# A planner that counts SyncE's own time in an attention stage, and key page tables that borrow the room of later ones

## The chip, the cores and the metric

The kernel runs on one core of a Trainium2 chip. The time is device time of one launch, in microseconds (us), the median of several executions. A profiled execution is a separate one, recorded by the hardware profiler. The engines that the text names are TensorE (PE, with PEld for its weight loads), VectorE (DVE), ScalarE (ACT), GpSimd (POOL) and SyncE (SP), which issues most of the DMA transfers.

## What is computed

One inference step of a two-layer decoder trunk in float32: layer 0 mixes tokens by a Conformer convolution, layer 1 by stick-breaking attention, and each layer ends in a gated ConvFFN. There are 512 prompt tokens and 8 sequences of 4 new tokens each, whose past of 256 tokens lies in 16 pages of a key and value pool. The change touches only the attention:

```python
def stick_breaking_block(q, k, v, bias, q_start):
    z = jnp.einsum('bqhd,bkhd->bhqk', q, k) * (HEAD_DIM ** -0.5) + bias[None, :, None, None]
    valid = k_pos[None, :] < q_pos[:, None]
    log_fail = jnp.where(valid, jax.nn.log_sigmoid(-z), 0.0)
    after = lax.cumsum(log_fail, axis=3, reverse=True) - log_fail
    weights = jnp.where(valid, jnp.exp(jax.nn.log_sigmoid(z) + after), 0.0)
    return jnp.einsum('bhqk,bkhd->bqhd', weights, v)
```

It is called once for the prompt (512 queries against 512 keys, 16 heads of 64) and once for the new tokens (4 queries against 256 paged keys and 4 new ones, for each sequence). New key and value rows are outputs too.

## The kernel before

All activations stay in the chip's memory, channels on the 128 partitions. Each weight block is split into a high and a low float32r part, `whi` by ScalarE and `wlo` by VectorE, and multiplied in three passes: high with high, low with high, high with low.

**The attention stage** is one `Plan`. Code records operations with `plan.op(engine, cost, function, r=reads, w=writes, a=adds)`, and at the end `plan.run()` lists them: it keeps a modelled clock for each engine, and again and again takes the operation that can start first, with corrections for rank and urgency. The instructions are issued in that order, so the costs in the list decide what stands ahead of what on each engine; on the chip each engine then works strictly in this order and waits on semaphores. An operation on SyncE has two times in the model: its cost, after which its readers may start, and the time for which it holds SyncE, which is 0.7 us for every one of them.

What the stage records, for 8 pairs of heads c = 0 to 7:

- `keys(c, h)` and `values(c, h)`, for token halves h: projections (`project`, lines 2163 to 2165 of `weighted`, six matmuls for each quarter), which TensorE uses as filler. Key rows are transposed by VectorE (line 2207) into one of two buffers `kr`, and four transfers of SyncE store them (line 2212). Value rows go through TensorE (line 2193) and a copy (line 2225), and one transfer stores them (line 2228).
- `pair(c)`: the prompt's attention in units of 512 columns. A unit is: logits z on TensorE (line 2432), exponential on ScalarE (2438) into a buffer `e` of a ring of six, masking on GpSimd (2446), clamp on VectorE (2451), logarithm on ScalarE (2453), scans on VectorE (2462), exponential (2466), product on VectorE (2467), transposes on TensorE (2474) with copies (2477), and products with the values (2494).
- `page_logits(m)`, m = 0 to 3: one group of four key pages each. A page is loaded by SyncE in four transfers of 128 KB (`key_page`, line 2045) into one of three page buffers, transposed by VectorE (line 2283), and multiplied with placed queries `Qz` (line 2301). Pages 0 to 2 are there before the stage. The even pages' transposes go to `kt`, the odd pages' to `second`: two of the six `e` buffers.
- `decode_weights`, `sequence(n)`: the new tokens' weights over the pages, and their products with value pages, which GpSimd gathers (line 2050). `new_logits` and `new_weights` do the same for the 4 new keys, from tables `Qf` (queries placed by 32 copies of GpSimd, `place_f`, line 2082), `kn` (keys, line 2315) and `Zw`, `wn` (weights). `Qf` and `Zw` are zeroed before the stage; `place_f` is recorded near its start.

Weight blocks of 1 MB come through SyncE as well (line 361), each into one of two buffers, when VectorE has split the block that was there. Each transfer of SyncE also waits until the one eight places ahead of it on SyncE has landed, since eight completion semaphores are used in turn.

Of the kernel before, what the change touches and what calls it, by code (L numbers as in the profile page):

```python
# [9 lines left out]
F32 = mybir.dt.float32  # L10
# [7 lines left out]
P = 128  # L18
D = 1024
# [62 lines left out]
E_BUFS, S_BUFS = 6, 2  # L82
# [23 lines left out]
class Plan:  # L106
# [5 lines left out]
    def __init__(self, eager=EAGER, chain=0.0, shifts=""):  # L112
        self.eager = eager
        self.shifts = shifts

        self.chain = chain
        self.ops = []
        self.writes, self.adds, self.reads = {}, {}, {}
        self.rings = {}
        self.follows = {}  # L120
        self.lift, self.urgent = {}, {}
        self.forms, self.change = {}, 0.0
        self.fill = set()

    def op(self, eng, cost, fn, r=(), w=(), a=(), follows=None, lift=0.0, urgent=0.0, after=(), form=None):

# [34 lines left out]
        if form is not None:  # L161
            self.forms[i] = form
        return i

# [27 lines left out]
    def run(self):  # L192
# [24 lines left out]
        while any(ready.values()):  # L217
# [23 lines left out]
            last[eng] = i  # L241
            free[eng] = t + (cost if eng != "sp" else 0.7)
            for u in users[i]:
# [7 lines left out]
def tile_trunk(  # L251
# [1866 lines left out]
    new_s = xflat[:, 4 * D:4 * D + 2 * P]  # L2118
    Zw = va.tile([P, 4, P], F32, name="Zw")
    wn = va.tile([P, 4, P], F32, name="wn")  # L2120
    oacc = Zd
    dec = vw.tile([P, NC, 4, 8], F32, name="dec")
    kn = vw.tile([P, NC, NS], F32, name="kn")
    Qf = vw.tile([P, NC, 4 * NS], F32, name="Qf")
    pool.memset(Qf, 0.0)
    pool.memset(Zw, 0.0)
    kt = kT.rearrange("p c t -> p (c t)")[:, 4 * T:4 * T + NC * KW]
# [70 lines left out]
    def keys(c, h):  # L2198
# [15 lines left out]

        plan.op("sp", 7.0, store, r=[kr])

# [14 lines left out]
    def new_rows(src, r, dst):  # L2231
# [15 lines left out]
        plan.op("act", 0.35, lambda: act.copy(new_s, rows()[:, :2 * P]), r=[rows], w=["new", "Qz"])  # L2247
        plan.op("sp", 3.0, store, r=["new"])


    def page(i):

        t = plan.tile("page", PAGE_BUFS, lambda: page_t[i % PAGE_BUFS])
        if i < PAGE_BUFS:
            plan.op("held", 0.0, lambda: None, w=[t])
            return t
        if i < 2 * NB:
            plan.op("sp", 2.0, lambda: key_page(t(), i), w=[t, ("asked", i)])
        else:
            plan.op("pool", 1.05, lambda: gather(t(), i % (2 * NB), cv), w=[t, ("asked", i)])  # L2260
        plan.op(f"page{i}", 6.0 if i < 2 * NB else 4.0, lambda: None, r=[("asked", i)], w=[(t, 1)])
        return t

    zt = {}

    second = [sbuf("e", 1024, E_BUFS) for _ in range(2)]

    plan.op("first pages", 3.0, lambda: None, w=["pages"])

    def page_logits(m):  # L2270
# [7 lines left out]
        for odd in range(2):  # L2278
            for pg in range(2):
                t = page(4 * m + 2 * odd + pg)  # L2280

                def turn(t=t, pg=pg, odd=odd):
                    dve.transpose(second[pg]() if odd else kt[:, pg * D:(pg + 1) * D], t())

                plan.op("dve", 1.25, turn, r=[t, (t, 1), "pages"], w=[("ktq" if odd else "ktp", pg)],
                        a=[second[pg]] if odd else [])

        def logits():
            for odd in range(2):
                b = 2 * (m % 2) + odd  # L2290
                c0 = 32 * b - 16 * odd
                if odd:
                    parts = [(pg * P, P, second[pg]()) for pg in range(2)]
                else:
                    parts = [(0, KW, kt)]
# [8 lines left out]

        plan.op("pe", 1.72, logits, r=[(k, i) for k in ("ktp", "ktq") for i in range(2)] + ["Qz", *second], w=[z], form="c32")
        if m % 2:
# [216 lines left out]
    both_halves(keys, 1)  # L2523
    for bg in range(2):
        plan.op("pool", 5.0, lambda bg=bg: place_f(bg), a=["Qf"])
    both_halves(values, 0)
    for c in range(NC):
# [3 lines left out]
        if c == 2:  # L2531
            decode_weights()
        if c + 2 < NC:
            both_halves(keys, c + 2)
# [89 lines left out]
```

## Time and profile before

| | |
|---|---|
| Median of 3 runs (lowest, highest) | 1257.34 us (1256.36 to 1258.67) |
| The profiled execution's own time | 1256.83 us |
| Its span | 1255.1 us |
| Attention stage, logits of the first unit to the last pair | about 639.6 to 826.5 us |
| DMA over the span | 142.40 MB, mean 113 GB/s |
| Key page loads, q1 and SyncE | 64 transfers of 128 KB |

A row of a window has its start and end, its length, and the busy time of TensorE, its weight loads, VectorE, ScalarE and GpSimd with the number of instructions, then TensorE's granted clock, the DMA engines' busy share and GB/s. A row of a timeline has start, duration, engine, source line, operation, "out<-in" by the program's names, shapes and a count; in brackets stands how long the engine sat idle before it, and what released it. SPq is SyncE's queue of transfers. A row of the chain of waits is one piece of the chain that ended last.

### The profile page before, as it was taken

The numbers are of one execution on the slowest core, as the hardware profiler recorded it, in microseconds if no ns is written. First come the engines' busy times: TensorE is split into PE (matmuls) and PEld (weight loads), VectorE is DVE, ScalarE is ACT, GpSimd is POOL, SyncE is SP. The second block draws the span as 40 slices with busy tenths as digits, with TensorE's granted clock in tenths as the row PEclk, the third lists the DMA queues.
The fourth block names the chain that finished last, engine by engine and source line by source line (L and its number), as shares of the span: only waits on it lengthen the run. The fifth ranks groups of instructions, "written<-read, shape, count | busy, mean of one in ns | idle before, by whom it ended". The sixth has DMA issues, their size and how long they took to land.

```text
span 1255.1 us, 26652 instructions
## 1 busy us (share of the span) xinstructions
PE 1239.3 (99%) x10742; PEld 1187.2 (95%) x10742; DVE 1011.2 (81%) x1700; ACT 709.8 (57%) x1421; POOL 173.8 (14%) x363
## 2 busy tenths in 40 slices
PE   9999999999999999999999999999999999999997
PEld 8997699999999999999988888999999999999997
DVE  7999887988987886878969897646979987887863
ACT  7793584646655454445545887744636645455453
POOL 5000014111001000000242344000101001000000
PEclk9999999999999999999999999999999999999999
DMA  7455423123233233244379465232123232233121
GB/s 223 129 168 152 129 68 117 35 86 114 80 112 118 68 106 99 92 145 161 97 190 246 128 173 159 71 126 85 49 88 102 93 120 93 80 108 118 60 79 72
DMA packets 139661, 142.40 MB, mean 113 GB/s; under 512 B 24045, under 2 KB 132773, under 8 KB 139266
## 3 DMA queue, kind: packets, MB, share of 16 engines
q1 hardware_dynamic: 133134, 120.29, 32.1%
q0 software_dynamic: 6400, 20.41, 5.2%
q8 instruction: 84, 1.38, 0.5%
q14 instruction: 39, 0.32, 0.1%
q10 hardware_dynamic: 4, 0.01, 0.0%
HBM read 129.34 MB, written 12.18 MB: 113 GB/s over the span
## 4 chain that ended last, share of the span: by engine, by line
PE 81%; DVE 14%; DMA 2%; ACT 2%; issue 1%; SPq 0%; POOL 0%; DVEq 0%; ACTq 0%
PE acc L1635 5%; PE acc L1634 5%; PE acc L1633 5%; PE acc L759 4%; PE acc L760 4%; PE acc L761 4%; PE av L896 3%; DVE wlo L401 3%; PE av L1412 3%; PE av L1413 3%; PE av L1414 3%; PE tr L1413 3%; PE tr L1412 3%; PE tr L1414 3%; PE tr L1633 3%; PE tr L1635 3%
## 5 line engine op out<-in xcount | busy, mean ns | idle before, releaser
L398 ACT CAST whi<-raw 128x1024 fp32r<-128x1024 f32 (+2 forms) x247 | 224.7, 913 | 123.5 <-PE av L1413 24.8
L401 DVE TENSOR_TENSOR wlo<-raw,whi 128x1024 fp32r<-128x1024 f32 (+2 forms) x247 | 258.7, 1050 | 33.0 <-ACT whi L398 31.5
L759 PE MATMUL acc<-XH,whi 128*128 128x288 f32 (+1 forms) x384 | 112.7, 294 | 0.0
L761 PE MATMUL acc<-XH,wlo 128*128 128x288 f32 (+1 forms) x384 | 110.3, 287 | 0.9 <-DVE wlo L401 0.9
L760 PE MATMUL acc<-XL,whi 128*128 128x288 f32 (+1 forms) x384 | 110.3, 287 | 0.0
L1412 PE MATMUL av<-HH,whi 128*128 128x288 f32 (+1 forms) x280 | 83.2, 297 | 0.5 <-DVE xT L1735 0.5
L1413 PE MATMUL av<-HL,whi 128*128 128x288 f32 (+1 forms) x280 | 82.6, 295 | 0.0
L1635 PE MATMUL acc<-TH,wlo 128*128 128x272 f32 x288 | 82.6, 287 | 0.0
L1634 PE MATMUL acc<-TL,whi 128*128 128x272 f32 x288 | 82.6, 287 | 0.0
L1633 PE MATMUL acc<-TH,whi 128*128 128x272 f32 x288 | 82.5, 287 | 0.0
L1414 PE MATMUL av<-HH,wlo 128*128 128x288 f32 (+1 forms) x280 | 82.2, 293 | 0.0
L1682 ACT COPY G<-acc 128x272 f32<-128x272 f32 (+1 forms) x72 | 26.8, 372 | 93.8 <-PE acc L1635 93.8
L2163 PE MATMUL acc<-XH,whi 128*128 128x256 f32 (+1 forms) x264 | 79.7, 302 | 0.0
L1412 PE MATMUL tr<-HH,whi 128*128 128x256 f32 (+1 forms) x280 | 78.5, 280 | 0.0
L1413 PE MATMUL tr<-HL,whi 128*128 128x256 f32 (+1 forms) x280 | 78.4, 280 | 0.0
L1414 PE MATMUL tr<-HH,wlo 128*128 128x256 f32 (+1 forms) x280 | 78.3, 280 | 0.0
L2165 PE MATMUL acc<-XH,wlo 128*128 128x256 f32 (+1 forms) x264 | 75.7, 287 | 0.0
L2164 PE MATMUL acc<-XL,whi 128*128 128x256 f32 (+1 forms) x264 | 75.7, 287 | 0.0
L759 PEld LDWEIGHTS acc<-XH,whi 128*128 128x128 f32 x384 | 72.2, 188 | 1.4 <-issue 0.4
L761 PEld LDWEIGHTS acc<-XH,wlo 128*128 128x128 f32 x384 | 72.1, 188 | 1.1 <-DVE wlo L401 1.1
L760 PEld LDWEIGHTS acc<-XL,whi 128*128 128x128 f32 x384 | 72.2, 188 | 0.3
L1573 DVE SCALAR_TENSOR_TENSOR cv<-G,fprm,cv 128x560 f32<-128x560 f32 x88 | 69.5, 797 | 0.5
(464 smaller groups left out, 4343.0 us busy)
## 6 DMA issues: line engine op xcount, KB each, us to landing
raw<-in_ffn_w_gate_dram SPq DMA_DIRECT2D x22, 1024.0 KB
raw<-in_ffn_w_up_dram SPq DMA_DIRECT2D x22, 1024.0 KB
raw<-in_ffn_w_down_dram SPq DMA_DIRECT2D x24, 768.0 KB
raw<-in_attn_w_qkv_dram SPq DMA_DIRECT2D x12, 1024.0 KB
xT<-in_cache_k_dram SPq DMA_DIRECT2D x64, 128.0 KB
raw<-in_conv_w_in_dram POOLq DMA_DIRECT2D x6, 1024.0 KB, 6.8
rep<-glu SPq DMA_DIRECT2D x36, 142.0 KB
raw<-in_conv_w_out_dram POOLq DMA_DIRECT2D x4, 1024.0 KB, 6.4
```

Source lines behind the costliest of these rows:

```text
L398: act.copy(hi[:, k, :], src[:, k])
L401: dve.tensor_tensor(lo[:, k, :], src[:, k], hi[:, k, :], op=ALU.subtract)
L759: pe.matmul(o, hi[:, k, :], XH[:, k, c0:c0 + n], start=(k == 0), stop=False)
L760: pe.matmul(o, hi[:, k, :], XL[:, k, c0:c0 + n], start=False, stop=False)
L761: pe.matmul(o, lo[:, k, :], XH[:, k, c0:c0 + n], start=False, stop=(k == NC - 1))
L1412: pe.matmul(o, hi[:, j + k, :], xh, start=(start and k == 0), stop=False, **kw)
L1413: pe.matmul(o, hi[:, j + k, :], xl, start=False, stop=False, **kw)
L1414: pe.matmul(o, lo[:, j + k, :], xh, start=False, stop=(stop and k == len(xs) - 1), **kw)
L1633: pe.matmul(o, hi[:, j + k, :], xh, start=(start and k == 0), stop=False, **kw)
L1634: pe.matmul(o, hi[:, j + k, :], xl, start=False, stop=False, **kw)
L1635: pe.matmul(o, lo[:, j + k, :], xh, start=False, stop=(k == 3), **kw)
L2163: pe.matmul(o, hi[:, k, :], XH[:, k, c0:c0 + n], start=(k == 0), stop=False)
```

## The change

SyncE's operations get a holding time of their own, `hold`: 2.1 us for a key page, 2.0 for a key row store, 1.9 for the store of new rows, with two of the costs changed too (7.0 to 6.5, 3.0 to 4.0). `Zw` and `wn` become two halves of one table, and the odd key pages' transposes go to that table and to `Qf` in place of two `e` buffers. `Qf` and `Zw` are therefore zeroed, and `Qf` filled, only after the last pages' logits have read them.

```diff
-    def op(self, eng, cost, fn, r=(), w=(), a=(), follows=None, lift=0.0, urgent=0.0, after=(), form=None):
+    def op(self, eng, cost, fn, r=(), w=(), a=(), follows=None, lift=0.0, urgent=0.0, after=(), form=None, hold=0.7):
...
+        self.hold[i] = hold
...
-            free[eng] = t + (cost if eng != "sp" else 0.7)
+            free[eng] = t + (cost if eng != "sp" else self.hold[i])
...
-    Zw = va.tile([P, 4, P], F32, name="Zw")
-    wn = va.tile([P, 4, P], F32, name="wn")
+    Zw_wn = va.tile([P, 8, P], F32, name="Zw_wn")
+    Zw, wn = Zw_wn[:, 0:4, :], Zw_wn[:, 4:8, :]
...
-    pool.memset(Qf, 0.0)
-    pool.memset(Zw, 0.0)
...
-        plan.op("sp", 7.0, store, r=[kr])
+        plan.op("sp", 6.5, store, r=[kr], hold=2.0)
...
-        plan.op("sp", 3.0, store, r=["new"])
+        plan.op("sp", 4.0, store, r=["new"], hold=1.9)
...
-            plan.op("sp", 2.0, lambda: key_page(t(), i), w=[t, ("asked", i)])
+            plan.op("sp", 2.0, lambda: key_page(t(), i), w=[t, ("asked", i)], hold=2.1)
...
-    second = [sbuf("e", 1024, E_BUFS) for _ in range(2)]
+    second = [Zw_wn.rearrange("p a r -> p (a r)"), Qf.rearrange("p k r -> p (k r)")]
...
-                    dve.transpose(second[pg]() if odd else kt[:, pg * D:(pg + 1) * D], t())
-
-                plan.op("dve", 1.25, turn, r=[t, (t, 1), "pages"], w=[("ktq" if odd else "ktp", pg)],
-                        a=[second[pg]] if odd else [])
+                    dve.transpose(second[pg] if odd else kt[:, pg * D:(pg + 1) * D], t())
+
+                plan.op("dve", 1.25, turn, r=[t, (t, 1), "pages"], w=[("ktq" if odd else "ktp", pg)])
...
-    for bg in range(2):
-        plan.op("pool", 5.0, lambda bg=bg: place_f(bg), a=["Qf"])
     both_halves(values, 0)
...
             decode_weights()
+            plan.op("pool", 1.0, lambda: pool.memset(Qf, 0.0), w=[("ktq", 1), "Qf"])
+            plan.op("pool", 0.7, lambda: pool.memset(Zw, 0.0), w=[("ktq", 0)] + [("Zw", i) for i in range(4)])
+            for bg in range(2):
+                plan.op("pool", 5.0, lambda bg=bg: place_f(bg), a=["Qf"])
```

The list that comes out is another one from the first unit on, on every engine, with the same operations in it; line numbers rise by two up to line 2116 and differ by little behind it. First, SyncE and VectorE where key pages 3 to 8 come in. SyncE before (one page is four pairs of an address computation and a load; their repeats are left out):

```order
L2045 ISA
L2045 DMA xT<-in_cache_k_dram 32x4x256
...
L2212 DMA out_dram<-kr_8353 32x8x32 x4
L361 DMA raw_8377<-in_attn_w_qkv_dram 128x8x256
L2212 DMA out_dram<-kr_8364 32x8x32 x4
...
L2212 DMA out_dram<-kr_8455 32x8x32 x4
L2212 DMA out_dram<-kr_8502 32x8x32 x4
```

SyncE now, from the same page loads (3 and 4) on; page 5 stands between the weights and the stores:

```order
L2047 ISA
L2047 DMA xT<-in_cache_k_dram 32x4x256
...
L363 DMA raw_8341<-in_attn_w_qkv_dram 128x8x256
...
L2212 DMA out_dram<-kr_8317 32x8x32 x4
L2212 DMA out_dram<-kr_8332 32x8x32 x4
```

Behind these two stores five pages (6 to 10) follow with no store between them, and no further store comes before page 15, the last. Before, page 5 and 6 stood behind the second store, then came two stores, pages 7 to 10, a fifth store, and the rest.

VectorE before, from the transposes of key rows on (`e_8421` takes page 3, `kT` pages 4 and 5, then `e_8338` page 6):

```order
L2207 STREAM_TRANSPOSE kr_8364<-kT 128x256
L401 TENSOR_TENSOR wlo_8362<-raw_8157,whi_8361 128x1024
L2283 STREAM_TRANSPOSE e_8421<-xT 128x1024
L2207 STREAM_TRANSPOSE kr_8455<-kT 128x256
L401 TENSOR_TENSOR wlo_8449<-raw_8200,whi_8448 128x1024
L2207 STREAM_TRANSPOSE kr_8502<-kT 128x256
L2451 TENSOR_SCALAR e_8467<-e_8467 128x1024
L2283 STREAM_TRANSPOSE kT<-xT 128x1024 x2
L2225 COPY vtok_8238<-one_8514 128x256
L2462 SCALAR_TENSOR_TENSOR s_8512<-ones,s_8512 128x512
L2283 STREAM_TRANSPOSE e_8338<-xT 128x1024
```

VectorE now, from the same place (`Qf` takes page 3, `Zw_wn` page 6; `e_8365` is the first unit, `e_8452` the second):

```order
L2207 STREAM_TRANSPOSE kr_8332<-kT 128x256
L403 TENSOR_TENSOR wlo_8326<-raw_8157,whi_8325 128x1024
L2450 TENSOR_SCALAR e_8365<-e_8365 128x1024
L2283 STREAM_TRANSPOSE Qf<-xT 128x1024
L2461 SCALAR_TENSOR_TENSOR s_8397<-ones,s_8397 128x512 x2
L403 TENSOR_TENSOR wlo_8416<-raw_8200,whi_8415 128x1024
L2283 STREAM_TRANSPOSE kT<-xT 128x1024 x2
L2450 TENSOR_SCALAR e_8452<-e_8452 128x1024
L2466 TENSOR_TENSOR e_8365<-e_8365,s_8397 128x1024
L2225 COPY vtok_8238<-one_8513 128x256
L2461 SCALAR_TENSOR_TENSOR s_8507<-ones,s_8507 128x384
L2283 STREAM_TRANSPOSE Zw_wn<-xT 128x1024
```

The first unit's clamp, scans and product have moved ahead of pages 4 to 6, and the third and fourth transposes of key rows have gone behind all pages. Between page 6's transpose and page 7's there now stand three scans and two clamps.

Second, TensorE from the first page group's logits to the first unit's transposes. Projection matmuls (line 2163 and the next two) stand between these rows and are left out. Before, 48 of them stand ahead of the first row, 30 each ahead of the second line-2193 group and of line 2474, and the second page group comes 6 projections and one z group later:

```order
L2301 MATMUL dz_8477<-kT,xT 32x256 x8
L2301 MATMUL dz_8477<-e_8338,xT 32x128 x4
L2193 MATMUL one_8514<-ident,vT_8505 128x128 x2
...
L2193 MATMUL one_8580<-ident,vT_8573 128x128 x2
...
L2474 MATMUL t_8641<-ident,e_8467 128x128 x4
```

Now 30 projections and a z group stand ahead of it, then 24, 6, 18 and 12 between the rows, and the second page group (last row) comes behind both halves of the first unit's transposes:

```order
L2300 MATMUL dz_8426<-kT,xT 32x256 x8
L2300 MATMUL dz_8426<-Zw_wn,xT 32x128 x4
L2193 MATMUL one_8513<-ident,vT_8504 128x128 x2
L2473 MATMUL t_8523<-ident,e_8365 128x128 x4
L2473 MATMUL t_8535<-ident,e_8365 128x128 x4
L2193 MATMUL one_8579<-ident,vT_8572 128x128 x2
...
L2300 MATMUL dz_8426<-kT,xT 32x256 x8
```

Between the two page groups there are 66 projections before and 60 now; over the whole stage their runs number 49 in both.

Third, GpSimd where the queries for the new keys are placed. Before, at the start of the stage (`kn` is the table of new keys, the maskings are those of the first two units):

```order
L2126 MEMSET Zw 128x512
L2082 COPY Qf<-qT 32x2x4x4 x32
L2315 COPY kn<-kT_s 32x32 x8
L2446 AFFINE_SELECT e_8467<-e_8467 128x2x128
L2446 AFFINE_SELECT e_8536<-e_8536 128x2x128 x2
```

Now, behind the last key page's transpose, among the value gathers (`e_9055` and `e_9278` are units of the third and fourth pair):

```order
L2052 DMA xT<-in_cache_v_dram,idx 128x1024
L2530 MEMSET Qf 128x1024
L2445 AFFINE_SELECT e_9055<-e_9055 128x2x128 x2
L2084 COPY Qf<-qT 32x2x4x4 x32
L2531 MEMSET Zw_wn 128x512
L2445 AFFINE_SELECT e_9278<-e_9278 128x2x128
L2052 DMA xT<-in_cache_v_dram,idx 128x1024 x2
```

The block of 32 copies has moved from ahead of the first masking to between two maskings of later units, behind the third gather of a value page.

More of the change, by code (lines that the diff above doesn't have):

```diff
@@ L123, in __init__ @@
         self.fill = set()
-    def op(self, eng, cost, fn, r=(), w=(), a=(), follows=None, lift=0.0, urgent=0.0, after=(), form=None):
+        self.hold = {}
+    def op(self, eng, cost, fn, r=(), w=(), a=(), follows=None, lift=0.0, urgent=0.0, after=(), form=None, hold=0.7):
         i = len(self.ops)
@@ L2292, in logits @@
                 if odd:
-                    parts = [(pg * P, P, second[pg]()) for pg in range(2)]
+                    parts = [(pg * P, P, second[pg]) for pg in range(2)]
                 else:
@@ L2303, in logits @@
                                       start=(b == e == 0), stop=(b == 3 and e == 1), skip_group_check=True)
-        plan.op("pe", 1.72, logits, r=[(k, i) for k in ("ktp", "ktq") for i in range(2)] + ["Qz", *second], w=[z], form="c32")
+        plan.op("pe", 1.72, logits, r=[(k, i) for k in ("ktp", "ktq") for i in range(2)] + ["Qz"], w=[z], form="c32")
         if m % 2:
```

## The prediction

> **What bounds the kernel now.** I read the engine totals first, then the stretches of the attention stage, then TensorE's waits, then the chain of waits. The first row is the page's, the next four are windows of the trace (the span of each, then busy time and instructions of each engine, granted clock, DMA share, GB/s).
>
> ```profile
> PE 1239.3 (99%) x10742; PEld 1187.2 (95%) x10742; DVE 1011.2 (81%) x1700; ACT 709.8 (57%) x1421; POOL 173.8 (14%) x363
> 639.60:696.00 56.40, 53.55 (x529) 47.48 (x528) 43.65 (x54) 27.48 (x51) 19.37 (x58) 1.00 0.91 219
> 696.00:780.00 84.00, 83.64 (x811) 69.43 (x811) 74.11 (x102) 70.38 (x118) 37.44 (x47) 1.00 0.52 154
> 780.00:826.50 46.50, 45.82 (x555) 41.07 (x553) 29.12 (x53) 32.00 (x65) 2.82 (x9) 1.00 0.33 89
> 826.50:833.00 6.50, 6.20 (x52) 5.95 (x50) 2.49 (x8) 1.52 (x5) 0.42 (x2) 1.00 0.53 225
> ```
>
> TensorE is busy 99% of the span at full clock, so the kernel takes the sum of its matmuls plus its waits. The order outside the attention stage does not change, so only the four stretches count. TensorE idles 56.40 - 53.55 = 2.85 us while the key pages come in, then 0.36, 0.68 and 0.30 us. All of it is 4.2 us, or 0.33% of the time: that is the most that better order can win, and it is little more than the 0.2% (2.5 us) that a measurement of this kernel can tell from no change. The waits by name (total, times, longest):
>
> ```profile
> PE t L2474 <- DVE e L2467: 1.4, 1, 1.4
> PE one L2193 <- ACT vT_s L2223: 1.4, 1, 1.4
> PE t L2474 <- ACT e L2477: 0.7, 1, 0.7
> PE one L2193 <- ACT vT L2221: 0.4, 1, 0.4
> ```
>
> Both long ones lie at 655 and 662 us. The chain of waits says what they come from:
>
> ```profile
> 640.11 5.27 DMA xT<-in_cache_k_dram
> 645.40 0.63 SPq L2212
> ...
> 647.20 4.65 DMA out_dram<-kr
> 652.08 0.27 issue
> 652.35 0.66 DVE e L2451
> ...
> 661.09 1.39 DVE e L2467
> 662.52 0.66 PE t L2474 x4
> ```
>
> A page load lands 5.27 us after its issue; only then does SyncE issue a key row store at 645.40, eight transfers behind that load. The store lands at 651.85, VectorE's next key row transpose waits for it, and the clamp L2451 of the first attention unit stands behind that transpose. So the table of 0.7 us for any SyncE operation hid a real cost, and the change addresses the right place.
>
> **The change, part by part.** *The counted time.* These are SyncE's issues and, last, the time from issue to landing of the page loads:
>
> ```profile
> 637.14 4.73 SPq L2045 DMA_DIRECT2D xT<-in_cache_k_dram  x8
> 642.06 2.22 SPq L2212 DMA_DIRECT2D out_dram<-kr  x4
> 656.98 6.05 SPq L2045 DMA_DIRECT2D xT<-in_cache_k_dram  x12
> DMA to landing us min/median/max: 4.5/5.4/7.7
> ```
>
> A page (four loads) holds SyncE 4.73 / 2 = 2.4 us, or 6.05 / 3 = 2.0; a key row store 2.2. The new 2.1 and 2.0 fit, and this part costs nothing by itself. What it does is order. No transfer is added; SyncE merely defers the stores, three of them past the last page.
>
> *The tables.* Odd pages no longer take two of the six "e" buffers, so the first units start without waiting for them, and the 32 copies of new queries into Qf leave the start of the stage. They held GpSimd for 9.77 us (row below), and the first unit's masking came behind them:
>
> ```profile
> 646.87 0.41 POOL L2446 TENSOR_SCALAR_AFFINE_SELECT e<-e 128x256 f32<-128x256 f32 x1 [0.27 <-POOL kn L2315]
> 640.00:650.00 10.00, 10.00 (x110) 8.21 (x106) 3.92 (x5) 3.06 (x7) 6.09 (x24) 1.00 1.11 258
> ```
>
> The clamp of that unit can now stand ahead of page 3's transpose instead of at 652.35, some 9 us earlier. VectorE was busy 3.92 of the 10 us from 640, so this work is hidden there.
>
> *TensorE's own work.* Over the stage each group of matmuls is still there once, and the number of runs of projection matmuls (49) is the same, so I take no change in the sum, with 0.1 us per moved group either way as a bound (some ten groups: 1 us). Prices come from the distances between these starts, and from the chain of waits:
>
> ```profile
> 636.75 0.28 PE L2163 MATMUL acc<-XH,whi 128*128 128x256 f32 x1
> ...
> 639.64 1.13 PE L2432 MATMUL z<-kT,qT 64*128 64x512 f32 x4
> 640.70 0.40 PE L2163 MATMUL acc<-XH,whi 128*128 128x288 f32 x1
> ...
> 643.97 0.28 PE L2163 MATMUL acc<-XH,whi 128*128 128x256 f32 x1
> ...
> 646.86 1.07 PE L2301 MATMUL dz<-kT,xT 128*32 128x256 f32 x16
> ...
> 665.04 1.87 PE dz L2301 x48
> ...
> 696.08 1.87 PE dz L2301 x48
> ```
>
> 24 projection matmuls take 2.9 us (256 columns) or 3.3 us (288), a group of logits z 1.06 us, the logits of one page group 1.87 us. The first page group is to start after 30 matmuls and a z group, at 640.70 + 3.3 + 0.7 + 1.06 = 645.8, 1.1 us sooner. It needs page 3's transpose, which ended at 644.03 + 1.25 = 645.28: no wait.
>
> From its end (647.6) to the second page group, before, lay 665.04 - 648.7 = 16.3 us with 2.85 of waits, so 13.5 of work. The new order has six projections fewer there (-0.7) and four transposes more (about +0.4): 13.2 us, so TensorE arrives at 660.8. Is VectorE done with page 7 by then?
>
> ```profile
> 644.03 1.25 DVE L2283 STREAM_TRANSPOSE e<-xT 128x1024 f32<-128x1024 f32 x1 [2.91 <-DMA xT<-in_cache_k_dram]
> ...
> 663.55 2.39 DVE L2462 TENSOR_TENSOR_SCAN s<-ones,s 128x384 f32<-128x384 f32 x4
> L2283 DVE STREAM_TRANSPOSE e<-xT 128x1024 f32<-128x1024 f32 x7 | 8.6, 1233 | 5.2 <-DMA xT<-in_cache_k_dram 5.2
> L401 DVE TENSOR_TENSOR wlo<-raw,whi 128x1024 fp32r<-128x1024 f32 x6 | 7.2, 1203 | 0.0
> L2467 DVE TENSOR_TENSOR e<-e,s 128x1024 f32<-128x1024 f32 x4 | 5.1, 1268 | 0.0
> L2451 DVE TENSOR_SCALAR e<-e 128x1024 f32<-128x1024 f32 x4 | 2.6, 662 | 0.0
> ```
>
> SyncE first, with no more than eight transfers under way. Pages 3 and 4 as before, to 641.9; the weights at 642.1; page 5's loads one by one as page 3's land, 642.7 to 644.5; the first store behind page 4's landings, 645.4 to 647.4; the second behind page 5's, 648.2 to 650.0; page 6 behind the first store's landings (4.65 us each), 650.6 to 652.2. At 5.2 us, between the shortest and the median, page 6 has landed by 657.4. On VectorE then come its transpose (1.23), three scans (2.39 less the first, 1.5), two clamps (1.32) and page 7's transpose (1.23): 662.7. **TensorE waits 1.9 us at the second page group.** The bounds are 0, if VectorE finds page 6 as soon as it is through with its earlier work (about 654.4, so 659.7 for page 7), and 4, if page 6 takes the longest 7.7 us. I take 1.9, since 5.2 is nearest to the rows of this stretch. The first unit's transposes cost about 0.2 us more (TensorE is there at 652.8, after a z group and 30 projections; the product, behind page 5's transpose at 651, a clamp and its own 1.27, ends at 653). That is 2.1 for 2.85: **-0.75 us**.
>
> [...]
>
> The third and fourth page groups have slack by the same count: the fourth comes to about 694.2, for 696.08, with about 0.9 us of TensorE work moved behind it. Two terms then remain. **The third pair's transposes** stand 15.8 us of TensorE work behind the fourth page group, at 710.0; on VectorE their product has 25 instructions ahead of it after page 15's transpose (692.5 to 693). At the mean of the stretch, 74.11 / 102 = 0.73 us, it ends at about 711.5; summed by its own kinds, nearer 709.5. Bounds 0 and 1.5, taken 0.4. **The moved Qf block** needs rows of GpSimd:
>
> ```profile
> 634.88 9.77 POOL L2082 COPY Qf<-qT 32x32 f32<-32x32 f32 x32
> 666.76 4.85 POOL L2077 COPY xT<-qT 32x32 f32<-32x32 f32 x16
> ...
> 693.10 0.70 POOL L2315 COPY kn<-kT_s 32x32 f32<-32x32 f32 x3 [6.46 <-DMA xT<-in_cache_v_dram,idx]
> ...
> 762.70 2.55 POOL L2315 COPY kn<-kT_s 32x32 f32<-32x32 f32 x4
> ```
>
> Copies behind a value gather wait for its landing (6.46 us at 693.10); the block now stands behind the third gather, which needs page 15's transpose. So 31 copies begin at about 692.7 + 6.5 = 699.2. At 0.31 us each (9.77 / 32) they end at 708.7, at 0.64 (2.55 / 4) at 719.0; 0.9 us for the fill of Zw and one masking follow. VectorE wants that masking after 31 instructions, at 692.5 + 31 x 0.73 = 715. I take 0.42 a copy, between the 0.30 of 666.76 and 0.64: done by 713.1, no cost. Bounds 0 and 4.9.
>
> Sum: -0.75 + 0.4 = -0.35 us; the 0.36, 0.68 and 0.30 stay, since the order behind the new logits is nearly the same and the last unit's chain does not shift against TensorE. The profiled run took 1256.83 us (span 1255.1), so 1256.5; it lies 0.5 below the median of 1257.34, so **1257.0 us** in the median.
>
> **Rivals.** *A, all the planned waits go (0.29).* Pages 6 and 7 find the DMA queues emptier, with three stores gone from the stretch, where the DMA share is 0.91, and VectorE, some 6 us ahead in its work, is not late again. For it: the 12 loads from 656.98 were issued 0.5 us apart, so the ninth at 661.0 had the first landed after 4.1 us. Then 2.85 + 0.36 go: 1257.34 - 3.2 = **1254.1 us**, faster.
>
> *B, the moved block is late (0.15): slower.* It decides from about 0.5 us a copy on; at 0.64 the masking comes at 719.9 against 715, VectorE stalls, and TensorE, whose next transposes have some 0.5 us of slack, loses 4.4: **1261.4 us**. For it: VectorE is busy 74 of 84 us in that stretch. Against it: the 16 copies at 666.76 ran at 0.30 us with VectorE full. The Trainium skill speaks for it: "SBUF — State Buffer", section "SBUF: two separate sides", says that VectorE and GpSimd share one port pair under an exclusive lock for a whole instruction. The trace agrees in part, with copies of 0.20 us and one of 1.19:
>
> ```profile
> L2082 POOL COPY Qf<-qT x32: 201/205/1187, 634.9 to 644.4; 32x32 f32<-32x32 f32 x32
> ```
>
> *C, the counted time is not the one that limits (0.10).* What paces SyncE is the landing eight transfers back, not 2.1 us of issue. If pages 6 and 7 take 7.7 us, the second page group waits 4.2 instead of 1.9, and VectorE carries some of it to the third: -0.35 + 2.5 + 0.7 is +2.9, **1260.2 us**.
>
> **How the numbers follow.** Forecast 0.46, A 0.29, B 0.15, C 0.10. Faster by over 0.2%: A and 0.02 of the forecast, 0.31. Slower: B and C, 0.25. Within: 0.44. The likeliest case alone spans the bounds of its terms, 1255 to 1259.3. The range takes in A with the 0.68 and some of the moved groups' gain (1253.2), and C and most of B (1261.2); about 2 in 10 is left out.
>
> **What would show it.** In the profile after: the clamp of the first unit before 645 us and no key row wait at 649 to 652 (if it is still there, the counted time failed); the second page group near 662.7 with a wait on L2283 of about 2 us (none: A; 4 and more: C); VectorE without a masking wait of over 1 us near 715 (more: B), and the 32 copies over 20 us there. I am wrong altogether if TensorE's idle time in the stage stays but the time moves, since then the sum of its matmuls changed with the order.

## The result, and the profile after

The changed kernel takes **1265.89 us** (median of 5 runs, 1265.47 to 1268.40) beside 1257.47 for the kernel before in the same session: ratio 1.0071, 95% interval 1.0059 to 1.0083. That is slower by 8.4 us and lies outside the predicted range of 1253.2 to 1261.2. The profiled execution of the changed kernel has a span of 1264.2 us, 9.1 more than before.

First the engine totals of the page, and two windows of the trace after (the first two of the four stretches that the prediction shows; columns as there):

```profile
PE 1243.0 (98%) x10742; PEld 1190.0 (94%) x10742; DVE 1010.7 (80%) x1700; ACT 709.7 (56%) x1421; POOL 174.7 (14%) x363
639.60:696.00 56.40, 52.98 (x514) 45.62 (x513) 48.68 (x56) 34.51 (x57) 16.57 (x38) 0.97 0.87 210
696.00:780.00 84.00, 80.05 (x775) 66.81 (x774) 62.67 (x92) 60.03 (x105) 44.45 (x78) 0.98 0.57 164
```

Two things are new. TensorE idles 3.42 us in the first stretch (2.85 before) and 3.95 in the second (0.36 before), and its granted clock, 1.00 everywhere before, is 0.97 and 0.98 there. So its busy time grew by 3.7 us although it has the same 10742 matmuls. The first logits z of the stage start at 640.73, 1.09 us later than before. That part of the 9.1 is no sign of the new order: `before_b5` below, which differs from the kernel before only behind that point, has its first z at 640.63.

The waits of TensorE by name (total, times, longest):

```profile
PE t L2473 <- DVE e L2466: 3.4, 1, 3.4
PE t L2473 <- ACT e L2476: 2.9, 2, 2.2
PE acc L499 <- DVE xT L2578: 1.3, 1, 1.3
PE av L2493 <- ACT qT L2508: 1.3, 1, 1.3
```

**Place 1, 654 to 657 us.** The 3.4 us come in front of the first unit's transposes. The chain of waits leads back from them (start, duration, what):

```profile
638.47 5.07 DMA xT<-in_cache_k_dram
643.60 7.96 DMA raw<-in_attn_w_qkv_dram
...
651.94 2.54 DMA out_dram<-kr
...
656.28 1.15 DVE e L2466
657.47 0.66 PE t L2473 x4
658.13 1.75 PE z L2431 x4
```

The same place on SyncE's queue and on VectorE, as timelines (in brackets the engine's idle time and what ended it):

```profile
643.60 0.40 SPq L363 DMA_DIRECT2D raw<-in_attn_w_qkv_dram  x1
644.19 2.03 SPq L2047 DMA_DIRECT2D xT<-in_cache_k_dram  x4
646.45 8.46 SPq L2212 DMA_DIRECT2D out_dram<-kr  x8
655.16 8.14 SPq L2047 DMA_DIRECT2D xT<-in_cache_k_dram  x16
```

```profile
643.73 0.69 DVE L2450 TENSOR_SCALAR e<-e 128x1024 f32<-128x1024 f32 x1 [1.27 <-POOL e L2445]
...
654.46 1.25 DVE L2283 STREAM_TRANSPOSE kT<-xT 128x1024 f32<-128x1024 f32 x1 [3.17 <-DMA out_dram<-kr]
...
656.20 1.21 DVE L2466 TENSOR_TENSOR e<-e,s 128x1024 f32<-128x1024 f32 x1
```

Page 5 is the row of four loads at 644.19, right behind the 1 MB weight block of 643.60. VectorE can take it only at 654.46: the last load, issued near 645.9, needed some 8.5 us where the median load needs 5.4. The first unit's product (656.20) stands behind page 5's transpose in VectorE's list, so TensorE, there at 654.05, waits until 657.47. The trace names the key row store as what ended VectorE's wait, since it landed last, but a page's transpose does not read it. SyncE's own queue says that it was the page: the last transfer of the stores, which stands eight places behind page 5's last load and so waits for its landing, was issued at 654.46 too. The store itself shows a second effect: the eight transfers of the two key row stores are spread over 8.46 us, because each transfer waits for the one eight places ahead of it, and for one of them that was the weight block.

**Place 2, 715 to 731 us.** GpSimd first, then VectorE:

```profile
698.61 1.95 POOL L2314 COPY kn<-kT_s 32x32 f32<-32x32 f32 x3 [3.82 <-DMA xT<-in_cache_v_dram,idx]
700.84 0.97 POOL L2052 DMA_INDIRECT xT<-in_cache_v_dram,idx  x1 [0.27 <-POOL kn L2314]
...
705.11 13.29 POOL L2084 COPY Qf<-qT 32x32 f32<-32x32 f32 x31 [0.49 <-DMA xT<-in_cache_v_dram,idx]
...
719.05 0.41 POOL L2445 TENSOR_SCALAR_AFFINE_SELECT e<-e 128x256 f32<-128x256 f32 x1
...
727.04 0.69 POOL L2314 COPY kn<-kT_s 32x32 f32<-32x32 f32 x3 [3.93 <-DMA xT<-in_cache_v_dram,idx]
727.81 0.76 POOL L2445 TENSOR_SCALAR_AFFINE_SELECT e<-e 128x256 f32<-128x256 f32 x2
```

```profile
719.49 0.69 DVE L2450 TENSOR_SCALAR e<-e 128x1024 f32<-128x1024 f32 x1 [4.35 <-POOL e L2445]
...
728.60 0.69 DVE L2450 TENSOR_SCALAR e<-e 128x1024 f32<-128x1024 f32 x1 [4.38 <-POOL e L2445]
```

The third value gather is issued only at 700.84, behind copies of new keys that waited for the second one's landing. The 31 copies of the Qf block behind it hold GpSimd until 718.4, and the masking that VectorE wants at 715.15 comes at 719.05: VectorE stalls for 4.35 us. Two value gathers were queued behind the block; the copies of new keys behind those wait 3.93 us for their landing, the next maskings stand behind these copies, and VectorE stalls for 4.38 us again. TensorE loses 2.2 and 1.3 us there.

Inside the block the copies do not run at one rate. These are two windows, while VectorE still works and while it stalls (GpSimd is the last engine ahead of the clock):

```profile
711.60:715.10 3.50, 3.50 (x40) 2.99 (x38) 3.50 (x6) 3.43 (x9) 3.29 (x6) 1.00 0.34 89
715.10:718.40 3.30, 3.30 (x32) 2.68 (x25) 0.04 (x1) 1.89 (x4) 2.76 (x14) 1.00 0.00 0
```

Beside VectorE's scans and the split of a weight block 6 copies ran in 3.50 us; once VectorE stood still, 14 ran in 3.30. So VectorE seems to slow the block that it then waits for; no run takes this apart.

**The clock.** Windows of 4 us after, at both places (the third number from the end is the granted clock):

```profile
656.00:660.00 4.00, 2.53 (x9) 0.92 (x10) 2.97 (x5) 1.74 (x3) 0.00 (x0) 0.80 0.90 217
660.00:664.00 4.00, 4.00 (x27) 4.00 (x27) 4.00 (x7) 2.78 (x6) 0.41 (x1) 0.78 1.13 216
...
720.00:724.00 4.00, 2.20 (x16) 2.20 (x17) 4.00 (x6) 3.53 (x7) 2.55 (x3) 0.90 0.53 142
724.00:728.00 4.00, 4.00 (x31) 3.66 (x33) 0.22 (x1) 1.43 (x2) 0.80 (x4) 0.67 0.76 188
```

Each pair gives up (0.20 + 0.22) x 4 and (0.10 + 0.33) x 4, that is **1.7 us** each time: 3.4 us at half clock. The z group at 658.13 shows it in one row, 1.75 us where it took 1.06 before. Before the change TensorE idled 1.4 us twice near the first place and the clock stayed at 1.00.

### The profile page after: what moved, and what is told of

Read it like the earlier page. It is cut to its first block, busy times and chain, and to the rows that moved or that the text cites. A ratio compares the mean times of both kernels' runs of the same rounds, so it can differ in the third digit from the quotient of the medians.

```text
span 1264.2 us, 26652 instructions
## 1 busy us (share of the span) xinstructions
PE 1243.0 (98%) x10742; PEld 1190.0 (94%) x10742; DVE 1010.7 (80%) x1700; ACT 709.7 (56%) x1421; POOL 174.7 (14%) x363
## 4 chain that ended last, share of the span: by engine, by line
PE 76%; DVE 14%; DMA 4%; issue 2%; ACT 2%; POOL 2%; SPq 0%; DVEq 0%; POOLq 0%; ACTq 0%
PE acc L1637 5%; PE acc L1636 5%; PE acc L1635 5%; PE acc L761 4%; PE acc L762 4%; PE acc L763 4%; PE av L898 3%; DVE wlo L403 3%; PE av L1414 3%; PE av L1415 3%; PE av L1416 3%; PE tr L1635 3%; PE tr L1637 3%; PE tr L1636 3%; PE tr L1415 3%; PE tr L1414 3%
```

## The experiments

Theory T: two causes, page 5 late in front of the first unit, and GpSimd late in front of VectorE, each with a stretch at half clock behind it; the new order as such costs nothing. Every kernel ran beside the kernel before on the same chip.

### Each half of the change alone

`hold_only` is the kernel before with the holding times and the two changed costs, and the tables as before. `tables_only` is the change without them:

```diff
-            free[eng] = t + (cost if eng != "sp" else self.hold[i])
+            free[eng] = t + (cost if eng != "sp" else 0.7)
...
-        plan.op("sp", 6.5, store, r=[kr], hold=2.0)
+        plan.op("sp", 7.0, store, r=[kr])
...
```

> The counted times alone, with the odd pages' transposes in e buffers and the Qf block at the start of the stage, as before. Theory T (two causes: page 5 lands late and holds VectorE's list, worth about 5 us with the loss of granted clock behind it; the moved Qf block holds GpSimd and then VectorE, worth about 4): the second cause cannot arise, the first only if page 5's loads stand behind the weight block with the first unit's product behind them, so 1258 to 1261. Rival H (the counted times do all the harm): 1265. Rival M (the order as such changes the sum of TensorE's matmuls): anything, with TensorE's idle time as before (4 us in the stage).

> The tables alone, with 0.7 us for every operation of SyncE. Theory T: the Qf block stands where it stands after the change, so its two VectorE stalls (about 4.4 us each near 719 and 728) are there; the two key row stores stand ahead of page 5 again, which then lands no sooner than after the change, so 1264 to 1268. Rival H (the counted times do the harm): 1258 to 1260, without the 3.4 us wait at the first unit's transposes.

Measured: `hold_only` 1262.35 us, ratio 1.0043 (1.0028 to 1.0057); `tables_only` 1268.35 us, ratio 1.0088 (1.0071 to 1.0105). Both halves cost time alone. The tables bring the place 2 of the change and, with 0.7 us a page, a wait of 4.2 us at place 1; the holding times in the change are no worse than none, and the intervals of 1.0088 and 1.0071 overlap. `tables_only` came 0.35 us above T's range, and `hold_only` 1.4 us: the latter by a third form of the same trouble, which I had not foreseen. Its rows on SyncE and VectorE:

```profile
642.54 0.40 SPq L363 DMA_DIRECT2D raw<-in_attn_w_qkv_dram  x1
643.13 2.00 SPq L2047 DMA_DIRECT2D xT<-in_cache_k_dram  x4
645.34 7.70 SPq L2214 DMA_DIRECT2D out_dram<-kr  x8
```

```profile
653.79 0.45 DVE L2209 STREAM_TRANSPOSE kr<-kT 128x256 f32<-128x256 f32 x1 [4.67 <-DMA out_dram<-kr]
```

Here the next key row transpose needs the buffer of a store that now stands behind the block and page 5, and TensorE waits 2.3 us behind it.

### One cause taken away at a time

`no_copies` leaves the 32 copies out of `place_f`; `page5_first` only changes when SyncE issues one weight block:

```diff
             dst = Qf[rows, :, 2 * NS * bg:2 * NS * (bg + 1)].rearrange("p (c q) (b r) -> p q c b r", q=4, b=4)[:, q, :, :, 4 * x:4 * x + 4]
-            pool.tensor_copy(dst, src)
```

```diff
             nc.sync.dma_start(out=t[32 * x:32 * x + 32, :].rearrange("p (q r) -> p q r", q=4), in_=pages[0, x])
+        if j == 4:
+            W.late = [0]
+        if j == 5:
+            n, W.late = len(W.late) - 1, []
+            for _ in range(n):
+                W.load()
```

(While `W.late` is not empty, `W.load()` only notes that a block is due.)

> The changed kernel's list with the 32 copies of new queries into Qf left out, so Qf stays zero and the new tokens' logits against the new keys are only the bias. Theory T: VectorE's two stalls behind GpSimd go, TensorE's waits of 2.2 and 1.3 us at 722 and 731 go with the clock loss between them, 4 us in all: 1261 to 1262.5, with granted clock 1.00 from 710 on, and the 3.4 us wait at 657 unchanged. Rival P (everything comes from the pages): 1265 to 1266. Rival M (the order's own sum): 1265 to 1266 too, though the waits go.

> The changed kernel's list with one change on SyncE: the weight block that stands ahead of page 5's four loads is issued behind them. Nothing else moves. Theory T: page 5 lands about 5 us after its issue, near 650, the 3.4 us wait at the first unit's transposes goes to under 0.5 and so does the clock loss behind it (z group at 1.06 us, not 1.75): 1260 to 1262. If only the wait itself counts and the clock has nothing to do with it: 1262.5. Rival Q (page 5 is late because of the page loads themselves, not the weight block): still a wait of 3 us or more, 1265 to 1266. Rival W (the weight block, now 2 us later, becomes what is waited for): a new wait on wlo or whi of 1 to 2 us, 1263 to 1264.

Measured: `no_copies` 1260.46 us, ratio 1.0023 (1.0013 to 1.0032): 5.4 us of the 8.4 are gone, more than T's 4, and the time lies 0.5 us below T's range. GpSimd and VectorE in it:

```profile
714.00 0.75 POOL L2444 TENSOR_SCALAR_AFFINE_SELECT e<-e 128x256 f32<-128x256 f32 x1 [11.39 <-ACT e L2436]
```

```profile
714.78 0.69 DVE L2449 TENSOR_SCALAR e<-e 128x1024 f32<-128x1024 f32 x1 [0.30 <-POOL e L2444]
...
723.77 0.69 DVE L2449 TENSOR_SCALAR e<-e 128x1024 f32<-128x1024 f32 x1 [3.80 <-POOL e L2444]
```

The first stall went with the block. The second, behind the new key copies that wait for the gathers, is still 3.80 us, but VectorE was early enough for it to cost TensorE only 1.1, and the clock stays at 1.00 from 664 us on. The 3.4 us at place 1 are unchanged, and here the trace names the page load itself for VectorE's wait in front of page 5's transpose (3.51 us, to 653.85).

`page5_first` took 1265.43 us, ratio 1.0060 (1.0043 to 1.0077): no gain that can be told from the change itself, where T promised 4 to 6. The time lies in rival Q's range, but Q's wait is not there: the wait did go. VectorE and TensorE's waits in it:

```profile
648.67 2.36 DVE L2293 STREAM_TRANSPOSE kT<-xT 128x1024 f32<-128x1024 f32 x2
...
658.32 1.25 DVE L2293 STREAM_TRANSPOSE Zw_wn<-xT 128x1024 f32<-128x1024 f32 x1 [4.37 <-DMA xT<-in_cache_k_dram]
```

```profile
PE t L2483 <- ACT e L2486: 3.5, 2, 2.8
PE av L2503 <- ACT qT L2518: 3.2, 1, 3.2
PE dz L2310 <- DVE Qf L2293: 2.0, 1, 2.0
```

Pages 4 and 5 are transposed back to back at 648.67, so page 5 had landed by 649.9 instead of 654.4, with nothing changed but the block's place: **the block made it late**. (Its loads, now ahead of the block, also go out 1.8 us sooner; the rest is a faster landing.) TensorE then works without a pause to 661. But page 6, behind the key row stores, comes only at 658.32; TensorE, earlier now, waits 2.0 us at the second page group and falls to half clock there, and 2.8 and 3.2 us at place 2, whose time hangs on the last pages and gathers and had moved little (its 31 copies began at 703.47, 1.6 us sooner). What was won at the first wait was paid at the next two.

### The pages ahead, with and without the copies

`pages_ahead` adds one more move on SyncE: the two key row stores go out behind page 7. `ahead_nocopies` also leaves the copies out.

```diff
         def store():
+            held_rows.append(stored) if held_rows else stored()
+
+        def stored():
             for a in range(4):
...
```

> The changed kernel's list with SyncE's issues alone moved: page 5 ahead of the weight block, and pages 6 and 7 ahead of the weight block's follower, the two key row stores, which go out behind page 7. Theory T, mended after the run with page 5 alone (its wait went, and 2 us came back at the second page group, where page 6 landed as late as ever behind the stores): both page waits are under 0.5 us and the granted clock is 1.00 up to 700. But the Qf block on GpSimd begins when the third value gather lands, behind page 15, so the masking behind it comes only 2 to 3 us sooner while VectorE and TensorE are 5 us sooner: its stalls grow, and 1262 to 1264 is left. Rival E (what is won at the pages is kept): 1260 to 1261. Rival Q (the page loads are late whatever stands ahead): a wait of 2 us or more on a page transpose again, 1265.

> The same move of SyncE's issues and the 32 Qf copies left out (Qf stays zero, so the new tokens' logits against the new keys are only the bias). Theory T: both causes are gone, and what is left of the change's cost is 1 us at the stage's end: 1255 to 1258, TensorE idle under 4 us in the stage, clock 1.00 throughout. Rival M (a part of the loss lies in the order itself): 1259 to 1261 with the waits gone.

Measured: `pages_ahead` 1263.87 us, ratio 1.0046 (1.0030 to 1.0063); `ahead_nocopies` **1257.81 us, ratio 1.0005** (0.9996 to 1.0015). Both times lie in T's ranges. In the first the page waits are small (1.0 us at the most, where T had 0.5) and place 2 has grown, waits of 3.1 and 2.5 us with half clock twice. GpSimd in it:

```profile
701.31 13.25 POOL L2102 COPY Qf<-qT 32x32 f32<-32x32 f32 x31 [0.53 <-DMA xT<-in_cache_v_dram,idx]
715.22 0.41 POOL L2466 TENSOR_SCALAR_AFFINE_SELECT e<-e 128x256 f32<-128x256 f32 x1
```

The masking is 3.8 us sooner than in the change, but VectorE is as much sooner and TensorE 4.8 us (fourth page group at 692.98 for 697.75): VectorE's stalls are 4.34 and 5.37 us, no less than in the change. In `ahead_nocopies` VectorE still stalls 4.12 us behind the gathers, which costs TensorE 1.6, and TensorE idles 4.44 us in the stage, where T had under 4. With the late page and the copies gone the order of the changed kernel is as fast as the one before: rival M, a loss in the order itself, is out, within 0.15%.

### The clock by itself

`idles` is the kernel before with eight holes in TensorE's work far from the attention stage:

```diff
                 o = pt()[:, :n]
+                if l == 0 and j == 4 and not start:
+                    turns.append(slot)
+                    for _ in range({8: 1, 13: 2, 18: 3, 23: 4, 28: 5, 33: 6, 38: 7, 43: 8}.get(len(turns), 0)):
+                        pool.tensor_copy(lo[:, 3:5, 0:64], lo[:, 3:5, 0:64])
...
```

> The kernel before with eight holes made in TensorE's work in the gated network of the first layer, where it otherwise has none: at eight places, far apart, GpSimd copies a piece of a split weight block onto itself 1, 2, ... 8 times between two groups of matmuls, which wait for it. Theory T: holes of up to about 2 us cost their own length; holes of 3.5 us and more, and some between 2 and 3.5 by where they fall, are followed by a stretch of 3.4 us at half clock (1.7 us lost), so the time is the 1257.4 of before, plus the sum of the holes, plus 1.7 times the number of such stretches. Rival L (the clock falls for another reason than the hole): clock 1.00 behind all of them and the sum of the holes alone.

Four of the holes as windows (length less the first busy time is the hole), and then the 4 us behind the last three:

```profile
238.00:242.00 4.00, 2.69 (x22) 2.49 (x21) 3.96 (x7) 3.08 (x4) 1.88 (x3) 1.00 0.00 0
...
368.00:373.00 5.00, 2.85 (x20) 2.64 (x19) 4.17 (x6) 2.92 (x5) 2.34 (x4) 0.90 0.00 0
...
420.00:425.00 5.00, 2.28 (x18) 2.05 (x17) 2.85 (x4) 0.30 (x1) 2.60 (x5) 1.00 0.00 0
...
503.00:509.00 6.00, 1.55 (x12) 1.35 (x12) 4.77 (x6) 2.01 (x3) 4.33 (x8) 0.96 0.00 0
```

```profile
371.00:375.00 4.00, 3.66 (x18) 3.66 (x19) 3.13 (x6) 1.23 (x3) 0.49 (x2) 0.62 0.12 17
...
424.00:428.00 4.00, 4.00 (x32) 4.00 (x33) 3.16 (x5) 1.05 (x1) 0.00 (x0) 1.00 0.00 0
...
508.00:512.00 4.00, 3.28 (x14) 3.28 (x15) 1.52 (x3) 1.27 (x3) 0.73 (x3) 0.57 0.00 0
```

Holes of 1.3 and 1.5 us left the clock alone; those of 2.15, 3.0, 3.1, 3.5 and 4.45 us were each followed by 3.4 us at half clock; the one of 2.72 us was not. In the attention stage of the same run an ordinary wait of 1.81 us was followed by such a stretch too. The holes sum to 21.7 us; with six stretches of 1.7 that makes 31.9, and the span grew by 1287.1 - 1255.1 = 32.0 (timed: 1290.65 us, ratio 1.0264, 1.0244 to 1.0285). Rival L is out.

The waits of the other profiles' attention stages fit in. Every wait there of up to 1.67 us left the clock alone, and every one of 3 us and more was followed by half clock. Between them it went both ways: waits of 2.03, 2.21, 2.23, 2.54 and, in `tables_only`, 2.60 us were followed by it; others of 2.33, 2.80 and, in `hold_b6`, 2.60 us were not. Behind 4.25 us in `tables_only` and 3.17 us in `page5_first` it lasted 6.8 us, two stretches.

### Versions that keep all the work

`split_ahead` is `pages_ahead` with the block recorded as eight planned operations of four copies. `hold_b6` and `before_b5` are `hold_only` and the kernel before with the weight block issued behind the two key row stores. `one_e_b6` has that too, gives only one odd page's transpose to the table of `Zw` and `wn` and the other to an `e` buffer, and fills `Qf` between the first maskings.

```diff
-            for bg in range(2):
-                plan.op("pool", 5.0, lambda bg=bg: place_f(bg), a=["Qf"])
+            for bg in range(2):
+                for part in range(4):
+                    plan.op("pool", 1.75, lambda bg=bg, part=part: place_f(bg, part), a=["Qf"])
...
```

> A version that keeps all of the work: SyncE's issues moved as before, and the two planned operations of 16 Qf copies (5.0 us each) made eight of four copies at 1.75 us each (0.43 us a copy, as measured), so that the planner can put maskings and gathers between them. This makes the list another one from there on. Theory T: VectorE has no wait on a masking of over 1.5 us near 720, TensorE no wait over 1.5 us, clock 1.00: 1255 to 1259. Rival G (GpSimd's copies are late however they are cut, since they still follow the third gather): VectorE waits of 2 us and more, 1261 to 1264.

> The kernel with the counted times alone, and one change on SyncE: the weight block that stands ahead of page 5 goes out behind the two key row stores. In the run without this move VectorE waited 4.67 us at 653.79 for a key row store, which SyncE had held back behind the landing of that block, and TensorE waited 2.3 us behind it. Theory T (the place of the 1 MB block among the small transfers decides): the store lands 2 to 3 us sooner, VectorE's wait is under 2.5 us, and 1262.35 becomes 1259 to 1260.5. Rival Q (the stores land late anyway): VectorE's wait 4 us or more and 1262. Rival W (the block comes too late for its first use by VectorE near 660): a wait on whi or wlo, 1261 to 1263.

> The kernel before with one change on SyncE: the weight block between the first two key row stores goes out behind the second. Theory T: the second store no longer stands behind the block, so it is issued up to 0.9 us sooner, and the 1.4 us wait at 655 shrinks by that; the later pages are as they were: 1256.2 to 1257.4 for 1257.8, hardly to be told from no change. Rival W (the block, now 2.5 us later, is late for its first use near 659): 1258 to 1259.

> A version that keeps the counted times and half of the table move: of the odd pages, one goes to the table of Zw and wn, the other to one e buffer; Qf is zeroed before the stage and filled in two pieces of 16 copies between the first maskings, behind the first page group, where GpSimd is idle; and the weight block goes out behind the two key row stores. Theory T: no Qf block stands behind the value gathers, so no VectorE wait on a masking of over 2 us near 715 to 730; no half-clock stretch; 1257 to 1260. Rival: the waits for key row stores and pages move to another place of VectorE's list, 1261 to 1263.

| kernel | time (us) | ratio to before | interval |
|---|---|---|---|
| split_ahead | 1260.77 | 1.0025 | 1.0014 to 1.0036 |
| hold_b6 | 1261.17 | 1.0028 | 1.0016 to 1.0040 |
| before_b5 | 1260.01 | 1.0018 | 1.0009 to 1.0027 |
| one_e_b6 | 1265.12 | 1.0056 | 1.0041 to 1.0071 |

None beats the kernel before, and T's range failed in all four; `before_b5` and `one_e_b6` lie above their rivals' ranges too. The planner put the eight pieces one behind the other again (31 copies in 14.31 us from 702.09 in `split_ahead`), and VectorE stalled 5.41 us: its stall and TensorE's waits are rival G's, its time lies just under G's range. In `hold_b6` VectorE's wait for the key row store went from 4.67 to 0.93 us, as T said, but 2.51 came back at page 6 (658.61), whose loads now stood right behind the block, and TensorE still waited 2.6 us; no wait on a weight block showed near 660, so it was not rival W, though the time lies in W's range. In `before_b5` it was page 5's turn to stand right behind the block, though T took the later pages to be as they were:

```profile
655.82 1.25 DVE L2293 STREAM_TRANSPOSE kT<-xT 128x1024 f32<-128x1024 f32 x1 [3.58 <-DMA xT<-in_cache_k_dram]
```

TensorE idles less in the stage of `before_b5` than in the kernel before (3.3 us for 4.2), yet one wait of 2.2 us was followed by half clock where two of 1.4 had not been, and that is part of its loss. `one_e_b6` has no Qf block at place 2 and stalls there all the same. GpSimd and VectorE in it:

```profile
721.07 0.70 POOL L2327 COPY kn<-kT_s 32x32 f32<-32x32 f32 x3 [4.04 <-DMA xT<-in_cache_v_dram,idx]
721.84 0.77 POOL L2458 TENSOR_SCALAR_AFFINE_SELECT e<-e 128x256 f32<-128x256 f32 x2
```

```profile
722.64 0.69 DVE L2463 TENSOR_SCALAR e<-e 128x1024 f32<-128x1024 f32 x1 [5.99 <-POOL e L2458]
```

That is the second half of place 2 alone: copies behind two gathers, maskings behind the copies. TensorE waits 4.1 us there. It also waits 3.0 us at 662.83, after VectorE had waited 2.73 us for page 6, which here too stands right behind the block.

## Why the prediction was wrong

The stage's own account, from 639 to 850 us of each profiled execution. Idle is the window's length less TensorE's busy time; a stretch at half clock is counted from windows of 4 us and costs 1.7 us.

| kernel | idle | stretches | sum | more than before | span more than before |
|---|---|---|---|---|---|
| before | 4.19 | 0 | 4.2 | | |
| after | 9.38 | 2 | 12.8 | 8.6 | 9.1 |
| hold_only | 7.32 | 0 | 7.3 | 3.1 | 4.4 |
| tables_only | 10.76 | 3 | 15.9 | 11.7 | 11.1 |
| no_copies | 6.69 | 1 | 8.4 | 4.2 | 3.7 |
| page5_first | 9.96 | 3 | 15.1 | 10.9 | 9.4 |
| pages_ahead | 9.54 | 2 | 12.9 | 8.8 | 7.6 |
| ahead_nocopies | 4.44 | 0 | 4.4 | 0.2 | 0.6 |
| split_ahead | 5.57 | 1 | 7.3 | 3.1 | 3.5 |
| hold_b6 | 5.85 | 0 | 5.9 | 1.7 | 3.7 |
| before_b5 | 3.32 | 1 | 5.0 | 0.8 | 1.4 |
| one_e_b6 | 8.29 | 2 | 11.7 | 7.5 | 8.3 |

Idle time and half clock together follow the spans to within 2 us. By the prediction's own steps:

- *Page 5's landing* was the step that failed first. "The product, behind page 5's transpose at 651" took about the stretch's usual 5.2 us for loads that are issued right behind a 1 MB block; the last one took 8.5. The 0.2 us at the first unit's transposes became 3.42 and 1.7 of clock. TensorE's arrival was right: 652.8 foretold, 654.05 measured, of which 1.09 is the late start. `page5_first` shows the block as the cause.
- *SyncE's row* failed by the same block. It had "the first store behind page 4's landings", but the fourth transfer of that store stands eight places behind the block: it waited 3.4 us and was issued at 651.58, and page 6's loads began at 655.16, where 650.6 was foretold.
- *The second page group's 1.9 us* did not appear, because TensorE came to it some 4 us late (666.28, where 660.8 and the late start of 1.09 make 661.9), when page 7's transpose had ended (664.9). The prediction's sign "none: A" would thus have read a second fault as a gain. In `page5_first`, where TensorE did not come late, the wait was 2.0; page 6 was late there too, so that the 1.9 was met is partly luck.
- *The Qf block*: rival B, put at 0.15. VectorE's need was right (715 foretold, 715.15 measured). The mean rate came out as taken (0.42 us a copy, 13.29 / 31 = 0.43 measured), but by luck: it mixes copies of about 0.58 us (3.50 / 6) beside VectorE's work with faster ones during its stall. The start was wrong, 699.2 foretold for 705.11, and with it the end of the masking, 713.1 for 719.46. The third gather was taken to go out right behind page 15's transpose and to land 6.5 us later. That transpose ended at 695.3, some 2.5 us late (1.1 of it the late start of the stage); the gather went out 5.5 us behind it, at 700.84, because GpSimd stood at copies that waited for the second gather; and the block went on 4.3 us later. B's point of decision, 0.5 us a copy, was worked out from the early start and so too high. B's stall of 4.4 us was met (4.35), but TensorE lost 2.2 us of it in waiting and 1.7 by the clock.
- *The gathers behind the block* were left out: behind the block, they put the new key copies' wait, and a second VectorE stall of 4.38 us, in front of the next maskings.
- *The price of a wait* was taken as its length: the clock was put at no cost, without a reason. Behind two of the waits came 1.7 us each at half clock. The Trainium skill, "TensorE: Matmul & The Clock Gate", section "Part 1: The HAM clock gate (the "warmup" mystery)", names a free-running activity window of about 3.4 us with half rate after an idle one; the length of the stretches here, 3.4 us, agrees. Behind every wait of 3 us and more in these stages there was such a stretch, so bounds of 4 us and more on a wait should have had it.
- *No change in the sum of TensorE's work* held: `ahead_nocopies` is within 0.15% of before. So did the count of VectorE's work from page 6's transpose to the end of page 7's (5.3 us foretold and measured), and the steps that the change was made for: the first unit's clamp came at 643.73 for "before 645", and the key row wait at 652 was gone.
- *One sum* is off: if page 6 takes 7.7 us in place of 5.2, the wait of 1.9 becomes 4.4, where the prediction gives 4 as the bound and 4.2 under C; C's time was added up with the right 2.5 more.

What stays open: `hold_only` and `hold_b6` lie 1.3 and 2.0 us above what their idle time explains; a late first z makes 0.3 and 1.1 of it, and the rest has no cause here. The executions of `hold_only` took 1261.20 to 1264.26 us, with a mean clock over the span of 0.998 down to 0.994; the profiled one, with no stretch at half clock, is the shortest, so the others may have had such stretches, which is not shown. Why copies of new keys, which read nothing of a value page, wait for a gather's landing was not examined. Whether the gain of the counted times could be kept with stores, pages and gathers in another order was not found. The cost of the stage's last wait (1.3 us at 840.96 for 0.3 before, behind a load of `xsave`) was not tried apart.

## What to carry to other kernels

When a wait is taken off an engine, ask of each transfer that moves up what it now stands behind, and price its landing by the largest transfer in flight (7.96 us for the block here, 8.5 for the load behind it), not by the median of its kind. A table that is lent out until late must be refilled late, and a refill on an engine that works in order delays everything queued behind it, the gathers and what waits for their landing too. The same idle time can cost different time: a single wait of about 2 us or more may bring TensorE to half clock (1.7 us more here), where two of 1.4 did not, so a new order is to be judged by its longest waits.

## What the runs showed of the hardware

- TensorE's granted clock halves for 3.4 us (1.7 us lost) behind a wait that can be as short as 1.81 us (`idles`), and need not behind one of 2.72 (`idles`) or 2.80 (`page5_first`). What decides between 1.81 and 2.80 us is not shown; that a window running by itself does, by where the wait falls in it, is a guess, and no window's edge was measured. The Trainium skill, "TensorE: Matmul & The Clock Gate", section "Why this matters for your kernels", asks for no gaps of more than about 3 us; the rows here show half clock behind shorter ones.
- A 128 KB load issued right behind a 1 MB load landed after 8.5 us, for 5.4 in the median, and the 1 MB load after 7.96. The same load ahead of the block landed within 5.8 us (`page5_first`).
- The same 32x32 copy on GpSimd took 0.30 us (9.77 / 32) in the mean early in the stage and 0.43 to 0.46 later. In the changed kernel's block it took about 0.58 us while VectorE ran scans and the split of a weight block (6 in 3.50 us) and about 0.24 while VectorE stood still (14 in 3.30). A busy VectorE alone does not make it slow: the 16 copies at 666.76 before took 0.30 us with VectorE full, mostly of transposes. Which of VectorE's instructions do it was not tried.
